# A residual block on one core: head blocks through the weight buffers, left columns first, three staggered chunks, later border transposes

## The chip, the core and the metric

One NeuronCore of a Trainium2 chip runs the whole block in one launch. The metric is the device time of one execution in microseconds. TensorE (PE in the profile) does matmuls and transposes, VectorE (DVE) and ScalarE (ACT) move, scale and convert, SyncE (SP) issues most DMAs, GpSimd (POOL) a few.

## What is computed

One layer for 256 tokens, model width 1024, all in float32 (the reference, cut):

```python
h = rmsnorm(x, ffn1_pre_g);  x = x + 0.5 * rmsnorm(swiglu(h, ffn1_w_in, ffn1_w_down), ffn1_post_g)
h = rmsnorm(x, mix_pre_g)
q_a, f_a, i_a, g_a, q_b, k_b, v_b, f_b, gates = split(h @ w_in)
o_a = rmsnorm(hgrn2_chunkwise(q_a, f_a, i_a), hg_norm_g) * silu(g_a)   # gated linear recurrence
o_b = fox_attention(q_b, k_b, v_b, f_b + fox_f_bias)                    # causal, forget gates
gate = sigmoid(gates + b_gate)
y = gate[0] * (o_a @ w_branch_a) + gate[1] * (o_b @ w_branch_b)
x = x + rmsnorm(y @ w_out, mix_post_g)
x = x + rmsnorm(mem_cross_attention(rmsnorm(x, mem_pre_g), rmsnorm(mem, mem_kv_g)), mem_post_g)
h = rmsnorm(x, ffn2_pre_g);  x = x + 0.5 * rmsnorm(swiglu(h, ffn2_w_in, ffn2_w_down), ffn2_post_g)
```

The inner width of each FFN is 2816, taken as 11 chunks of 256 (`NFF`).

## The kernel before

Every float32 operand of a large matmul is split into a rounded part `hi` (ScalarE cast, L122) and the rest `lo` (VectorE subtraction, L123), and each product is three matmuls: hi by hi, hi by lo, lo by hi. The weights are 261 units of 128 x 1024. `unit` loads one through SP into a `raw` buffer (four of them) and converts it into a pair `hi`/`lo` (eight pairs); it does so once and keeps the pair in a cache, so a pair stays held until its last matmul. `chunk` is four units, one 1024 x 512 piece of a matrix. `loads` lists the weight DMAs in the order they are written.

`proj_tok` multiplies 128 tokens (half `h`) by a chunk: 24 matmuls of 512 columns into one bank (tag `mm`, two banks). `rows_proj` and `down` accumulate a half of the tokens over rows of a weight into two banks of 512 columns each (tag `acc`, four banks); the results of `accs`, `po` are for token halves 0 and 1. The token halves go one after the other so that work on one lies under the matmuls of the other:

- `post` ends a sublayer for one half: sums of squares by ScalarE (`ssq`, L219), the product with the post gain (L279), an inverse root by an integer start value and Newton steps on 128 x 1 tiles (`rstd_of`, L203 to L210), and the update of `x` (L283).
- `half` follows it: eight PE transposes of the new `x` (`to_T`, L256), their gain and hi/lo split (`gain_split`, L247 and L248), and the pre-norm's inverse root. `half(X2, ...)` stands at the border from FFN 1 to the projections, `half(X3, ...)` from the mixer's output to the memory sublayer, `half(X4, ...)` from the memory output to FFN 2.
- In an FFN, `act_evac` makes a chunk's activations (L308, L310) and `flush` transposes and splits them (L303, L136, L137) for `down`. `STAG` is the number of last chunks whose `down` runs after all activations, half 0 and then half 1.

The tile framework orders each engine's queue by its own model of when operands are ready; the order then is fixed and each engine works it off in order. `after(i)` gives a block high priority but puts it on PE behind matmul number `i` of the list `log`; the constants `L_...` say how many matmuls behind the start of a stage. `issue_after` alone does this for one instruction, DMA issues included. These constants are lower limits: a block comes later if the model has it ready later.

At the head, x^T comes in five DMAs on ACT's queue into tiles of its own and the first four units through `unit` on SP's queue; `act_first` runs the first two FFN chunks for both halves, k-block by k-block, before the inverse root of `x` is known (`norm_1`). Seven matmuls on ones (`WARM`) run before data is there.

Of the kernel before, what the change touches and what calls it, by code (L numbers as in the profile page):

```python
# [16 lines left out]
P = 128  # L17
# [27 lines left out]
WARM = 7  # L45

X_AT = 6
# [18 lines left out]
def block_kernel(ctx: ExitStack, tc: tile.TileContext, wts, x_in, xT_in, mem_in, memT_in, cols, rows, fbias, masks, out):  # L66
# [46 lines left out]
    def unit(name, i, parts=1):  # L113
        u = _AT[name] + i
        if u not in cache:
            raw = wp.tile([P, D], F32, tag="raw", name=nm("raw"), bufs=4)
            hi = wp.tile([P, D], F32R, tag="hi", name=nm("hi"), bufs=8)
            lo = wp.tile([P, D], F32R, tag="lo", name=nm("lo"), bufs=8)
            for a in range(0, D, D // parts):
                cut = slice(a, a + D // parts)  # L120
                loads.append(nc.sync.dma_start(raw[:, cut], wts[u][:, cut]).ins)
                S.copy(hi[:, cut], raw[:, cut])  # L122
                V.tensor_tensor(out=lo[:, cut], in0=raw[:, cut], in1=hi[:, cut].bitcast(F32), op=ALU.subtract)  # L123
            cache[u] = (hi, lo)
        return cache[u]
# [74 lines left out]
    def rstd_of(s, scaled=True):  # L200

        v = s1(name="v")
        V.tensor_scalar(out=v, in0=s[:, 0:1], scalar1=s[:, 1:2], scalar2=D * EPS, op0=ALU.add, op1=ALU.add)  # L203
# [11 lines left out]
        V.tensor_scalar(out=r, in0=y, scalar1=-1.0 / 256.0, scalar2=None, op0=ALU.mult)  # L215
        return r
# [55 lines left out]
    def post(ps, h, grow, factor=1.0, last=False):  # L272

        s = s1(2, name="ss2")
        ts = []
        for j in range(2):
            ssq(s[:, j : j + 1], ps[j])
            t = sp.tile([P, 512], F32, tag="z2", name=nm("post"), bufs=3)
            V.scalar_tensor_tensor(out=t, in0=ps[j], scalar=-factor / 256.0, in1=grow[:, j * 512 : (j + 1) * 512], op0=ALU.mult, op1=ALU.mult)  # L279
            ts.append(t)  # L280
        r = rstd_of(s, scaled=False)
        for j, (t, xh) in enumerate(zip(ts, x_halves(h))):
            V.scalar_tensor_tensor(out=xh, in0=t, scalar=r, in1=xh, op0=ALU.mult, op1=ALU.add)  # L283
            if last:
                nc.sync.dma_start(out[h * P : (h + 1) * P, j * 512 : (j + 1) * 512], xh)


    def ffn(w_in, w_dn, X, r2, n_tok, i_row, first_half, second_half=None):
# [17 lines left out]
        def act_evac(ps, c, h):  # L306
            sg = sp.tile([P, FC], F32, tag="c1", name=nm("sg"), bufs=7)
            S.activation(sg, ps[:, :FC], AF.Silu, scale=r2[h])  # L308
            a = sp.tile([P, FC], F32, tag="c1", name=nm("at"), bufs=7)
            V.scalar_tensor_tensor(out=a, in0=ps[:, FC:], scalar=r2[h], in1=sg, op0=ALU.mult, op1=ALU.mult)  # L310
            ats[c, h] = a
            if h == 1:
                late.append(c)
# [19 lines left out]
        def down(c, h):  # L333
            act = acts[c]
            hs = slice(h * P, (h + 1) * P)
            for j in range(2):
                wh, wl = unit(w_dn, 2 * c + j)
                ah, al = act[:, 0, j, hs], act[:, 1, j, hs]
                for n in range(2):
                    ns = slice(n * 512, (n + 1) * 512)  # L340
                    for i, (a, w) in enumerate(((ah, wh), (ah, wl), (al, wh))):
                        MM(accs[h][n], a, w[:, ns], start=(c == 0 and j == 0 and i == 0), stop=(c == NFF - 1 and j == 1 and i == 2))
# [21 lines left out]
        for c in range(n_tok, NFF):  # L364
# [10 lines left out]
            while done < min(c - 1, NFF - STAG):  # L375
# [4 lines left out]
                done += 1  # L380
        m = len(log)
        for c in range(NFF - STAG, NFF):
            down(c, 0)
# [3 lines left out]
        for c in range(NFF - STAG, NFF):  # L387
            down(c, 1)
        if first_half:
            first_half(m)  # L390
            post(accs[1], 1, grow, 0.5)
        else:
            post(accs[1], 1, grow, 0.5, True)
# [4 lines left out]
    xT = [m4([P, 2, T + 1], n="xT") for _ in range(KB // 2)]  # L398
    for kb in range(2):
        S.dma_start(xT[0][:, kb], xT_in[:, kb])  # L400
    for j in range(1, 4):
        S.dma_start(xT[j], xT_in[:, 2 * j : 2 * j + 2])
# [350 lines left out]
    def gates(c):  # L753
# [3 lines left out]
        nc.sync.dma_start(brow, rows[4 + c // 2, c % 2 * 512 : c % 2 * 512 + 512].partition_broadcast(P))  # L757
# [43 lines left out]
    last = None  # L801
    for c in range(2):
        ua, ub = chunk("br_a", c), chunk("br_b", c)
        for h in range(2):
            za, zb = zs[c][:, h], zs[2 + c][:, h]
            m = len(log)
            pa = mm()
            proj_tok(pa, OA, ua, h)
            if last:
                y_T(*last, m + L_Y)  # L810
            V.tensor_tensor(out=za, in0=pa, in1=za, op=ALU.mult)
            pb = mm()
            proj_tok(pb, OB, ub, h)
            V.tensor_tensor(out=zb, in0=pb, in1=zb, op=ALU.mult)
            V.tensor_tensor(out=za, in0=za, in1=zb, op=ALU.add)
            last = c, h

    def rows_proj(ps, X, name, h, kbs):
        a, b = h * P, h * P + P
        for kb in kbs:  # L820
            wh, wl = unit(name, kb)
            for n in range(2):
# [8 lines left out]
    for h in range(2):  # L831
        rows_proj(po[h], Y, "w_out", h, range(0, 4))
        if h == 0:
            y_T(*last, m + L_Y)
# [5 lines left out]
    half(X3, r3, 0, G_MEM, m + L_WO)  # L840
# [5 lines left out]
    for c in range(2):  # L846
# [8 lines left out]
        if c == 0:  # L855
            half(X3, r3, 1, G_MEM, m + L_MK)
# [74 lines left out]
    for h in range(2):  # L931
        m = len(log)
# [14 lines left out]
def _layout(inputs):  # L947
# [41 lines left out]
    def col(v):  # L989
# [12 lines left out]
    )  # L1002
    r = {
        "wts": wts, "x": nat(a["x"]), "xT": np.concatenate([tra(a["x"]), col(a["ffn1_pre_g"][0])[:, :, None]], axis=2), "mem": nat(a["mem"]), "memT": tra(a["mem"]),
# [19 lines left out]
```

## Time and profile before

| | |
|---|---|
| runs | 807.54, 808.13, 808.2 us, median 808.13 |
| profiled execution | 807.36 us, span 805.6 us |
| granted TensorE clock, mean over the span | 0.997 |
| busy: PE, DVE, ACT | 98%, 65%, 51% of the span |
| HBM read | 146.02 MB, 183 GB/s over the span |
| a weight unit, 512 KB, from issue to landing | 4.3 us median |

The span runs from the first to the last instruction of the program that the profiler recorded; the execution's own time is a little longer. Rows of the timeline give start and duration in us, engine, source line, operation, output and inputs, shape and count; a bracket tells how long the engine sat idle before and what released it. Matmuls overlap, so a row's duration is not its share of the time: the distance between starts is.

### The profile page before, as it was taken

The page shows a single profiled execution, that of the slowest core. Times are in us where ns is not written, and L with a number is a line of the kernel's source. Part 1 is how long each engine was busy: PE and PEld are TensorE (multiplying, and loading weights), DVE is VectorE, ACT ScalarE, POOL GpSimd, SP SyncE. Part 2 cuts the span into 40 slices and gives each one's busy share as a digit, 9 for nine tenths or more (in the row PEclk, how much of TensorE's full clock was granted, in tenths as well). Part 3 has the DMA queues.
Part 4 walks back from the last instruction along what each step waited for, and adds up shares of the span by engine and source line. Part 5 has one row for each costly group of instructions (what it writes and reads, how often), then busy time and mean ns, then how long its engine had stood idle before and what let it go on. Part 6 is the DMA issues. An engine that isn't in the chain of part 4 may idle for free.

```text
span 805.6 us, 12769 instructions
## 1 busy us (share of the span) xinstructions
PE 792.6 (98%) x5040; PEld 679.4 (84%) x5040; DVE 525.1 (65%) x837; ACT 414.3 (51%) x623; POOL 9.2 (1%) x20
## 2 busy tenths in 40 slices
PE   8999999999999999999999999999999999999996
PEld 6888888888899889998888888999887788888884
DVE  6865545548776897678675666975659655545544
ACT  6754444537754435447674445645647654434531
POOL 0000000000000100200000000000000000000000
PEclk9999999999999999999999999999999999999998
DMA  8866654555455463643486555455425656665521
GB/s 331 302 223 209 211 200 157 193 173 183 164 203 171 171 195 123 212 155 120 139 291 235 177 161 201 146 197 196 151 77 186 210 185 206 209 201 166 182 79 52
DMA packets 41867, 147.90 MB, mean 184 GB/s; under 512 B 4808, under 2 KB 5200, under 8 KB 41808
## 3 DMA queue, kind: packets, MB, share of 16 engines
q1 hardware_dynamic: 40624, 144.46, 53.2%
q0 software_dynamic: 464, 1.58, 0.6%
q10 hardware_dynamic: 720, 1.05, 0.4%
q8 instruction: 39, 0.64, 0.3%
q14 instruction: 20, 0.16, 0.1%
HBM read 146.02 MB, written 1.06 MB: 183 GB/s over the span
## 4 chain that ended last, share of the span: by engine, by line
PE 89%; DVE 4%; DMA 2%; issue 2%; ACT 1%; SPq 0%; DVEq 0%; ACTq 0%
PE mm L80 63%; PE acc L80 23%; DMA raw<-in_wts_dram 2%; DVE lo L123 2%; PE tr L303 1%; PE tr L80 1%; ACT junk L219 1%; DVE xs L283 1%; PE tr L256 1%; DVE t L208 1%; DVE y L210 0%; ACT hi L122 0%; PE tr L712 0%; DVE post L279 0%; PE tr L901 0%
## 5 line engine op out<-in xcount | busy, mean ns | idle before, releaser
L123 DVE TENSOR_TENSOR lo<-raw,hi 128x1024 fp32r<-128x1024 f32 (+1 forms) x262 | 317.7, 1222 | 93.3 <-ACT hi L122 83.7
L122 ACT CAST hi<-raw 128x1024 fp32r<-128x1024 f32 (+1 forms) x262 | 270.8, 1047 | 140.0 <-PE mm L80 105.1
L80 PE MATMUL mm<-lo,hT 128*128 128x512 f32 x576 | 225.9, 392 | 0.0
L80 PE MATMUL mm<-hi,hT 128*128 128x512 f32 x576 | 225.6, 392 | 0.0
L80 PE MATMUL mm<-hi,lT 128*128 128x512 f32 x576 | 225.1, 391 | 0.1
L80 PEld LDWEIGHTS mm<-hi,lT 128*128 128x128 f32 x576 | 108.2, 188 | 23.0 <-DVE lT L248 0.8
L80 PEld LDWEIGHTS mm<-hi,hT 128*128 128x128 f32 x576 | 108.2, 188 | 22.6 <-ACT hT L247 0.5
L80 PEld LDWEIGHTS mm<-lo,hT 128*128 128x128 f32 x576 | 108.2, 188 | 21.7
L80 PE MATMUL acc<-hi,act 128*128 128x512 f32 x352 | 111.8, 391 | 0.0
L80 PE MATMUL mm<-hT,lo 128*128 128x256 f32 x392 | 111.3, 284 | 0.0
L80 PE MATMUL mm<-hT,hi 128*128 128x256 f32 x392 | 111.2, 284 | 0.0
L80 PE MATMUL mm<-lT,hi 128*128 128x256 f32 x392 | 111.1, 283 | 0.0
L80 PEld LDWEIGHTS acc<-hi,act 128*128 128x128 f32 x352 | 66.1, 188 | 13.4
L80 PEld LDWEIGHTS mm<-lT,hi 128*128 128x128 f32 x392 | 75.2, 192 | 0.1
L80 PEld LDWEIGHTS mm<-hT,hi 128*128 128x128 f32 x392 | 75.2, 192 | 0.1
L80 PEld LDWEIGHTS mm<-hT,lo 128*128 128x128 f32 x392 | 75.2, 192 | 0.1
L80 PE MATMUL acc<-lo,act 128*128 128x512 f32 x176 | 70.0, 398 | 0.0
L308 ACT ACTIVATE sg<-mm,rstd 128x256 f32<-128x256 f32 x40 | 19.0, 474 | 76.2 <-PE mm L80 76.2
L310 DVE SCALAR_TENSOR_TENSOR at<-mm,rstd,sg 128x256 f32<-128x256 f32 x40 | 19.2, 480 | 58.8 <-ACT sg L308 58.8
L80 PEld LDWEIGHTS acc<-lo,act 128*128 128x128 f32 x176 | 33.1, 188 | 6.4
L80 PE MATMUL acc<-hi,hT 128*128 128x512 f32 x96 | 35.5, 396 | 1.6 <-ACT hi L122 1.1
L80 PE MATMUL acc<-hi,lT 128*128 128x512 f32 x96 | 35.4, 396 | 0.5 <-DVE lT L248 0.5
(175 smaller groups left out, 630.2 us busy)
## 6 DMA issues: line engine op xcount, KB each, us to landing
raw<-in_wts_dram SPq DMA_DIRECT2D x260, 512.0 KB, 4.3
grow<-in_rows_dram SPq DMA_DIRECT2D x4, 512.0 KB, 5.8
brow<-in_rows_dram SPq DMA_DIRECT2D x4, 256.0 KB, 4.9
xs<-in_x_dram SPq DMA_DIRECT2D x2, 512.0 KB, 5.5
cbm<-cd POOLq DMA_DIRECT2D x2, 512.0 KB, 8.5
memT<-in_memT_dram SPq DMA_DIRECT2D x2, 512.0 KB, 7.5
ms<-in_mem_dram SPq DMA_DIRECT2D x2, 512.0 KB, 7.8
out_dram<-xs SPq DMA_DIRECT2D x4, 256.0 KB, 2.1
```

The source lines that it names most:

```text
L80: log.append(PE.matmul(*args, **kw).ins)
L122: S.copy(hi[:, cut], raw[:, cut])
L123: V.tensor_tensor(out=lo[:, cut], in0=raw[:, cut], in1=hi[:, cut].bitcast(F32), op=ALU.subtract)
L208: V.scalar_tensor_tensor(out=t, in0=v, scalar=y, in1=y, op0=ALU.mult, op1=ALU.mult)
L219: S.activation(junk[:, : src.shape[-1]], src, AF.Square, accum_out=dst)
L256: PE.transpose(ps[:, j * P : (j + 1) * P], src(kb), ident)
L283: V.scalar_tensor_tensor(out=xh, in0=t, scalar=r, in1=xh, op0=ALU.mult, op1=ALU.add)
L303: PE.transpose(trv[:, j, h * P : (h + 1) * P], ats[c, h][:, j * P : (j + 1) * P], ident)
L308: S.activation(sg, ps[:, :FC], AF.Silu, scale=r2[h])
L310: V.scalar_tensor_tensor(out=a, in0=ps[:, FC:], scalar=r2[h], in1=sg, op0=ALU.mult, op1=ALU.mult)
```

## The change

1. *Head.* x^T block, weight block and gain column of each of eight k-blocks stand side by side in a new input `head` (128 x 776 per block) and are loaded by eight DMAs on SP's queue through the four `raw` buffers. The unit list `wts` starts at unit 4. A block's `lo` is written behind its gain split. `WARM` is 8; the load of `x` moves behind another load (`X_AT`); the gate bias rows are loaded behind the gates' units.
2. *Inverse root.* Three Newton steps (six operations) become one Newton step and one of higher order (five), with another scale (`SC_RSTD`).
3. *FFN.* `STAG` is 3. For half 0 (and half 1 in FFN 2) the last chunks' `down` does columns 0 to 511 of all of them and then columns 512 to 1023. The flush in the first two chunks of FFN 2 goes; these chunks are flushed in chunk 2.
4. *The end.* `post_last`: ScalarE's square root and VectorE's reciprocal with one Newton step; the table of the square root is called for behind the last Silu; the last 512 columns are updated and stored in two pieces, one over ACT's queue.
5. *Branches.* `br_a` for both halves, then `br_b` for both halves, per 512 columns.
6. *Memory sublayer.* `half(X3, ...)` for half 0 moves from the end of the output projection into the key projection. The memory output does k-blocks 0 to 2 for both halves, then the rest of half 0 (left columns first), then the rest of half 1.
7. Larger `L_...` constants.

```diff
+SC_RSTD = 0.375
-STAG = 4
-L_ACT = 15
-L_F1 = 18
-L_IA = 22
-L_WO = 18
-L_MK = 46
-L_MO = 18
+STAG = 3
+L_ACT = 21
+L_F1 = 24
+L_IA = 36
+L_WO = 30
+L_MK = 84
+L_MO = 21
-WARM = 7
-X_AT = 6
+WARM = 8
+X_AT = 10
...
-        for c in (3.0, 12.0, 768.0):
-            t = s1(name="t")
-            V.scalar_tensor_tensor(out=t, in0=v, scalar=y, in1=y, op0=ALU.mult, op1=ALU.mult)
-            y2 = s1(name="y")
-            V.scalar_tensor_tensor(out=y2, in0=t, scalar=c, in1=y, op0=ALU.subtract, op1=ALU.mult)
-            y = y2
+        t = s1(name="t")
+        V.scalar_tensor_tensor(out=t, in0=v, scalar=y, in1=y, op0=ALU.mult, op1=ALU.mult)
+        z = s1(name="y")
+        V.scalar_tensor_tensor(out=z, in0=t, scalar=3.0, in1=y, op0=ALU.subtract, op1=ALU.mult)
+        t = s1(name="t")
+        V.scalar_tensor_tensor(out=t, in0=v, scalar=z, in1=z, op0=ALU.mult, op1=ALU.mult)
+        w = s1(name="t")
+        V.scalar_tensor_tensor(out=w, in0=t, scalar=40.0 / 3.0, in1=t, op0=ALU.subtract, op1=ALU.mult)
+        y = s1(name="y")
+        V.scalar_tensor_tensor(out=y, in0=w, scalar=80.0, in1=z, op0=ALU.add, op1=ALU.mult)
...
+    def post_last(ps, h, grow, factor):
+        s = s1(2, name="ss2")
+        ts = []
+        for j in range(2):
+            ssq(s[:, j : j + 1], ps[j])
+            if j == 0:
+                sums = s1(name="v")
+                V.tensor_scalar(out=sums, in0=s[:, 0:1], scalar1=D * EPS, scalar2=None, op0=ALU.add)
+            else:
+                y = s1(name="y")
+                S.activation(y, s[:, 1:2], AF.Sqrt, bias=sums)
+                v = s1(name="v")
+                V.tensor_tensor(out=v, in0=s[:, 1:2], in1=sums, op=ALU.add)
+            t = sp.tile([P, 512], F32, tag="z2", name=nm("post"), bufs=3)
+            V.scalar_tensor_tensor(out=t, in0=ps[j], scalar=-factor * 16.0, in1=grow[...], op0=ALU.mult, op1=ALU.mult)
+            ts.append(t)
+        z = s1(name="y")
+        V.reciprocal(z, y)
+        t = s1(name="t")
+        V.scalar_tensor_tensor(out=t, in0=v, scalar=z, in1=z, op0=ALU.mult, op1=ALU.mult)
+        r = s1(name="y")
+        V.scalar_tensor_tensor(out=r, in0=t, scalar=3.0, in1=z, op0=ALU.subtract, op1=ALU.mult)
+        for a, b, eng in ((0, 512, nc.sync), (512, 768, nc.scalar), (768, 1024, nc.sync)):
+            xh = xs[:, h, a:b]
+            V.scalar_tensor_tensor(out=xh, in0=ts[a // 512][...], scalar=r, in1=xh, op0=ALU.mult, op1=ALU.add)
+            eng.dma_start(out[h * P : (h + 1) * P, a:b], xh)
...
+            if c == NFF - 1 and h == 1 and not first_half:
+                with tc.issue_after(silu.ins):
+                    S.activation(warm, ones[:, 0:1], AF.Sqrt)
...
             for c in range(n_tok):
-                n = len(log)
                 act_tok(c, h)
-                flush(n + L_ACT)
...
-        for c in range(NFF - STAG, NFF):
-            down(c, 0)
+        for cut in (left, right):
+            for c in range(NFF - STAG, NFF):
+                down(c, 0, (cut,))
...
-    xT = [m4([P, 2, T + 1], n="xT") for _ in range(KB // 2)]
-    for kb in range(2):
-        S.dma_start(xT[0][:, kb], xT_in[:, kb])
-    for j in range(1, 4):
-        S.dma_start(xT[j], xT_in[:, 2 * j : 2 * j + 2])
+    heads = [wp.tile([P, D], F32, tag="raw", name=nm("head"), bufs=4) for _ in range(KB)]
+    for kb in range(KB):
+        loads.append(nc.sync.dma_start(heads[kb][:, : T + 512 + KB], head_in[kb]).ins)
...
-    for j in range(4):
-        unit("f1_in", j, 2 if j == 0 else 1)
-        for i in range(2):
-            gain_split(X1, 2 * j + i, xT[j][:, i, :T], xT[j][:, i, T:], first=2 * j + i == 0)
+    for kb in range(KB):
+        if kb % 2 == 0:
+            cache[_AT["f1_in"] + kb // 2] = parts_of()
+        hi, lo = (p[:, kb % 2 * 512 : kb % 2 * 512 + 512] for p in cache[_AT["f1_in"] + kb // 2])
+        w = heads[kb][:, T : T + 512]
+        S.copy(hi, w)
+        gain_split(X1, kb, heads[kb][:, :T], heads[kb][:, T + 512 + kb : T + 512 + kb + 1], first=kb == 0)
+        V.tensor_tensor(out=lo, in0=w, in1=hi.bitcast(F32), op=ALU.subtract)
...
-        nc.sync.dma_start(brow, rows[...].partition_broadcast(P))
+        with tc.issue_after(loads[-1]):
+            nc.sync.dma_start(brow, rows[...].partition_broadcast(P))
...
-    half(X3, r3, 0, G_MEM, m + L_WO)
...
-        if c == 0:
-            half(X3, r3, 1, G_MEM, m + L_MK)
+            if c == 0:
+                half(X3, r3, j, G_MEM, m + (L_WO, L_MK)[j])
...
-    for h in range(2):
-        m = len(log)
-        rows_proj(po[h], AO, "mo", h, range(0, 4))
-        rows_proj(po[h], AO, "mo", h, range(4, 8))
-        if h == 1:
-            half(X4, r4, 0, G_F2, m + L_MO)
-        post(po[h], h, g3)
+    for kb in range(3):
+        for h in range(2):
+            rows_proj(po[h], AO, "mo", h, (kb,))
+    for n in range(2):
+        rows_proj(po[0], AO, "mo", 0, range(3, KB), (n,))
+    post(po[0], 0, g3)
+    m = len(log)
+    rows_proj(po[1], AO, "mo", 1, range(3, KB))
+    half(X4, r4, 0, G_F2, m + L_MO)
+    post(po[1], 1, g3)
```

More of the change, by code (lines that the diff above doesn't have):

```diff
@@ L65, in block_kernel @@
 @with_exitstack
[L66 removed]
+def block_kernel(ctx: ExitStack, tc: tile.TileContext, wts, head_in, x_in, mem_in, memT_in, cols, rows, fbias, masks, out):
     nc = tc.nc
@@ L111, in block_kernel, with parts_of, unit @@
     loads = []
-    def unit(name, i, parts=1):
+    def parts_of():
+        return [wp.tile([P, D], F32R, tag=t, name=nm(t), bufs=8) for t in ("hi", "lo")]
+    def unit(name, i):
         u = _AT[name] + i
@@ L116, in unit @@
             raw = wp.tile([P, D], F32, tag="raw", name=nm("raw"), bufs=4)
[L117 to L123, printed above, removed]
+            hi, lo = parts_of()
+            loads.append(nc.sync.dma_start(raw, wts[u - 4]).ins)
+            S.copy(hi, raw)
+            V.tensor_tensor(out=lo, in0=raw, in1=hi.bitcast(F32), op=ALU.subtract)
             cache[u] = (hi, lo)
@@ L270, in load_row, with post @@
         return r
-    def post(ps, h, grow, factor=1.0, last=False):
+    def post(ps, h, grow, factor=1.0, store=False):
         s = s1(2, name="ss2")
@@ L386, in ffn @@
         m = len(log)
-        for c in range(NFF - STAG, NFF):
-            down(c, 1)
         if first_half:
+            for c in range(NFF - STAG, NFF):
+                down(c, 1)
             first_half(m)
@@ L821, in rows_proj @@
             wh, wl = unit(name, kb)
-            for n in range(2):
+            for n in cols:
                 ns = slice(n * 512, (n + 1) * 512)
```

66 lines of the change are left out of this document (38 added, 28 removed).

## The prediction

> **What bounds the kernel now.** I read the page first, then the chain in order of time, then the timeline of each stretch where TensorE is not back to back.
>
> ```profile
> span 805.6 us, 12769 instructions
> PE 792.6 (98%) x5040; PEld 679.4 (84%) x5040; DVE 525.1 (65%) x837; ACT 414.3 (51%) x623; POOL 9.2 (1%) x20
> ```
>
> TensorE carries the time. The chain shows its pace in a steady piece of the second FFN:
>
> ```profile
> 652.52 10.88 PE mm L80 x48
> 667.03 0.44 PE tr L303 x4
> ```
>
> 48 matmuls of 512 columns in 10.88 us are 0.227 us each, with no wait between. The change alters the number of real matmuls nowhere, so it can win only where PE waits: at the head, at the borders between stages, and behind the last matmul. It loses where it makes a new wait.
>
> **The head.** Eight k-blocks of x^T and weights are fetched; each wants six matmuls (1.36 us) in chunk 0.
>
> ```profile
> 1.68 1.73 ACTq L402 DMA_DIRECT2D xT<-in_xT_dram  x3
> 4.68 0.35 DVE L245 TENSOR_SCALAR hT<-xT 128x256 fp32r<-128x256 f32 x1 [3.66 <-DMA xT<-in_xT_dram]
> 4.84 0.60 ACT L122 CAST hi<-raw 128x512 fp32r<-128x512 f32 x1
> 5.49 0.72 PE L80 MATMUL acc<-hi,hT 128*128 128x512 f32 x2 [1.07 <-ACT hi L122]
> 6.56 0.51 ACT L247 ACTIVATE hT<-xT 128x256 fp32r<-128x256 f32 x1
> 6.69 0.69 DVE L123 TENSOR_TENSOR lo<-raw,hi 128x512 fp32r<-128x512 f32 x1 [0.53 <-ACT hi L122]
> 7.30 0.48 DVE L248 SCALAR_TENSOR_TENSOR lT<-xT,hT 128x256 fp32r<-128x256 f32 x1
> 29.59 0.39 PE L80 MATMUL mm<-hi,hT 128*128 128x512 f32 x1
> ```
>
> The first two chunks are 96 matmuls, 21.8 us at pace. They take 29.59 - 5.49 = 24.1 us, so 2.3 us are lost inside and the stream behaves as if it had started at 7.8 us.
>
> ```profile
> 0.00:14.00 14.00, 10.91 (x42) 7.92 (x43) 6.81 (x13) 8.06 (x14) 0.71 (x6) 1.00 0.84 308
> DMA to landing us min/median/max: 3.2/4.7/7.0
> ```
>
> These are the first 14 us by windows (last column GB/s) and the landing times of the weight tile in the first 60 us. A new block is 128 rows of 776 floats, 397 KB: 1.29 us at 308 GB/s, under the 1.36 us that PE needs for it. When does block 0 land? It is issued at about 0.75 like the first load now. The fastest 512 KB load took 3.2 us, so 3.95 is the early bound; the first piece of x^T and the first half unit, together about as many bytes, were in by 4.84, the late bound. I take 4.4. Per block ACT then has 0.60 + 0.51 = 1.11 us and DVE 0.48 + 0.69 = 1.17 us, both under 1.36. Followed through: block 0 makes PE start at 5.1; block 1 lands at 5.7, its hi and hT are done at 6.8, lT at 7.35, lo at 8.05, so its matmuls end at 8.5; from block 2 on (in at 7.0, ready at 8.1) PE is the slower party. Matmul 13 starting at 8.5 means an effective start of 8.5 - 12 x 0.227 = 5.8, against 7.8: 2.0 us. Blocks 4 to 7 must wait until a raw buffer is read out by lo (block 0: about 6.0) and need a fresh trip of about 3.2 us: in at 9.3, hT at 10.4, wanted at 11.2. Later ones have less air, so I book 0.2 us back: **head -1.8** (range -2.5 to 0). The extra warm-up matmul lies before the first landing: nothing. The bias row's transfer leaves the head for the gates stage: nothing, since its load there follows that chunk's last unit and its reader comes after 24 matmuls, 5.4 us.
>
> **The borders.** Each residual update (`post`) and its transposes must hide under the matmuls of the other token half.
>
> ```profile
> 172.60:181.20 8.60, 8.60 (x40) 7.13 (x39) 1.66 (x2) 0.59 (x1) 0.00 (x0) 1.00 0.46 158
> 182.20:204.90 22.70, 21.77 (x102) 17.39 (x101) 20.70 (x50) 15.05 (x30) 0.00 (x0) 1.00 0.56 186
> 589.00:597.10 8.10, 8.10 (x37) 6.71 (x36) 0.56 (x1) 0.00 (x0) 0.00 (x0) 1.00 0.05 20
> 597.15:621.00 23.85, 23.60 (x113) 19.41 (x112) 21.18 (x51) 17.69 (x35) 0.00 (x0) 1.00 0.52 177
> ```
>
> DVE (third number behind the length) idles before the border, 1.66 of 8.60 and 0.56 of 8.10 us, and is then the full engine, 20.7 of 22.7 and 21.2 of 23.9. The reason is the pool: eight hi/lo pairs are all held by the four staggered chunks (or by all of the memory output weights), so the next stage's conversions run only once the second half gives them back.
>
> ```profile
> L123 DVE TENSOR_TENSOR lo<-raw,hi 128x1024 fp32r<-128x1024 f32 x8 | 9.8, 1219 | 0.2 <-ACT hi L122 0.2
> L279 DVE SCALAR_TENSOR_TENSOR post<-acc,grow 128x512 f32<-128x512 f32 x4 | 2.8, 689 | 8.1 <-ACT junk L219 7.9
> 202.81 0.39 PE L80 MATMUL mm<-hi,lT 128*128 128x512 f32 x1
> 203.92 1.32 PE L256 MATMUL tr<-ident,xs 128*128 128x128 f32 x8 [0.72 <-DVE xs L283]
> 188.22 0.63 PE L256 MATMUL tr<-ident,xs 128*128 128x128 f32 x4 [0.20 <-issue]
> 503.58 0.63 PE L256 MATMUL tr<-ident,xs 128*128 128x128 f32 x4 [0.23 <-DVE xs L283]
> 603.94 0.63 PE L256 MATMUL tr<-ident,xs 128*128 128x128 f32 x4 [0.25 <-DVE xs L283]
> 621.89 0.40 PE L80 MATMUL mm<-lo,hT 128*128 128x512 f32 x1
> 624.80 0.40 PE L80 MATMUL mm<-lo,hT 128*128 128x512 f32 x1
> 636.57 0.39 PE L80 MATMUL mm<-lo,hT 128*128 128x512 f32 x1
> 637.64 0.44 PE L303 MATMUL tr<-ident,at 128*128 128x128 f32 x2 [0.69 <-DVE at L310]
> ```
>
> *FFN 1 to the projection.* Waits 0.20 and 203.92 - 202.81 - 0.23 = 0.88. Three staggered chunks shorten the second half from 48 to 36 matmuls: 12 x 0.227 = 2.7 us of cover gone. Off DVE go two of the eight `lo` (2 x 1.22, into the idle stretch), one of the first half's two `post` products (0.69, since its left 512 columns now finish 18 matmuls early) and one small operation in each of three root chains (0.22 each by the tail's rows below): 3.8 us. It comes out 1.1 us ahead: **-1.0** (range -1.1 to +2.7). *Memory border.* The transposes are put at least 30 matmuls into the key projection, its 192 matmuls being the cover: **-0.2** (0 to -0.25). *Memory output to FFN 2.* Waits 0.25, then nine steps in 2.91 us from 621.89 (0.87 lost behind the second half's splits), then 637.64 - 636.57 - 0.23 = 0.84 for an activation that DVE delivers late. Interleaving k-blocks 0 to 2 leaves 30 instead of 48 matmuls behind the first half, 4.1 us of cover gone; three `lo` (3.7), a `post` product (0.7) and the root chains (0.66) leave DVE's full stretch, 5.1. So the 0.25 goes and about 0.3 of the 0.87; the rest stays, since those transposes are still placed four matmuls before that cover ends. The flush at 637.64 moves a chunk later, behind 21 matmuls of new work, and its 0.84 goes: **-1.4** (-2.0 to +4.1).
>
> *Stagger and flush order:* chunk 7's down projection moves into the loop, the same matmuls. Left columns first leaves chunk 10's activations only 12 matmuls, 2.7 us, and its transposes as cover:
>
> ```profile
> 775.92 1.59 PE acc L80 x7
> 775.96 0.47 ACT L308 ACTIVATE sg<-mm,rstd 128x256 f32<-128x256 f32 x1 [0.33 <-PE mm L80]
> 777.81 0.59 ACT L136 CAST act<-tr 128x512 fp32r<-128x512 f32 x1 [0.44 <-PE tr L303]
> 616.84 1.28 ACT L308 ACT_TABLE_LOAD   x1 [2.92 <-DVE rstd L215]
> 618.14 0.47 ACT L308 ACTIVATE sg<-mm,rstd 128x256 f32<-128x256 f32 x1
> ```
>
> The cast is done at 778.4, 2.5 us after the tail's first matmul: it fits. In FFN 2 a square-root table load follows that `sg` (ends 776.43): 1.28 and a one-column warm-up (estimated 0.2 from the one-column read of 0.19 in the tail's rows) end at 777.9, 0.1 behind the cast's present start. Nothing (0 to +0.3 each).
>
> One piece of the branch stage in the chain:
>
> ```profile
> 450.36 10.93 PE mm L80 x48
> ```
>
> The branch stage now works weight by weight with the same matmuls and transposes. There PE runs at pace already (48 in 10.93 us), and four units at a time instead of eight leave more air: nothing, to -0.1.
>
> Against the table load the Trainium skill speaks: "ScalarE: Activation LUTs", What ACT_TABLE_LOAD costs, puts a switch at 1283 ns plus a drain of 1380 ns. The row here agrees with the first part and shows no drain behind it, the next activation starting 0.02 us after the load.
>
> **The tail.**
>
> ```profile
> 797.40 0.60 ACT L219 ACTIVATE junk<-acc 128x512 f32<-128x512 f32 x1 [9.51 <-PE acc L80]
> 798.61 0.19 ACT L219 ACTIVATION_READ_ACCUMULATOR junk<-acc 128x1 f32 x1
> 799.45 0.20 DVE L203 TENSOR_SCALAR v<-ss 128x1 f32<-128x1 f32 x1
> 801.22 1.42 DVE L283 SCALAR_TENSOR_TENSOR xs<-post,y,xs 128x512 f32<-128x512 f32 x2
> out_dram<-xs SPq DMA_DIRECT2D x4, 256.0 KB, 2.1
> ```
>
> The second half's sum is read at 798.80 either way, because it waits for the last matmul. Now DVE does `post`, then eight small operations from 799.45 to 801.2, then two updates until 802.64, and the last store leaves there. After: `post` as now, `v` and three small operations at about 0.22 us, while the square root runs on ACT beside `post`: updates from about 800.3. They come in 512, 256 and 256 columns, about 1.5 us, so the last store leaves at 801.8 and carries 128 KB instead of 256. That is 0.85 sooner, and 0 to 0.4 for the smaller store: **-1.0** (-0.6 to -1.3).
>
> **Sum.** Head 1.8, borders 1.0 + 0.2 + 1.4, tail 1.0: 5.4 us. The profiled execution took 807.36 us (span 805.6 and 1.8 around it); the median of the runs is 808.13. So 807.36 - 5.4 = 802.0 for that execution and, 0.77 above it, **802.7** for the median.
>
> **Rivals.** (1) *The raw ring paces the head.* Four buffers serve a block in trip + conversion. With the median trip of 4.7 instead of 3.2, block 4 is in at 10.7, ready at 11.9 instead of 11.2, and the next chunk's first unit a round later again behind; about 1.8 us return, and the time is 804.5. For it: the large trips of this stretch. Against: those had four x^T pieces and up to four units in flight at once, where now there are at most four smaller blocks. (2) *The cover is cut and DVE does not get lighter*, because the queue orders the next stage's conversions into the border all the same. Then 2.7 + 4.1 = 6.8 us of cover are missing, the waits of 0.88, 0.20, 0.25 and 0.87 stay, and head, tail, memory border and flush save 3.8: 811.1. It is slower by over 0.2% once more than 5.4 of the 6.8 come back. For it: DVE at nine tenths there, with 2.0 and 2.7 us of air. Against: two long idle stretches right before, with the loads free to come. (3) *The table switch holds ACT for two load lengths*, 2.56 us: the cast starts 1.4 late at 779.2 and is done at 779.8; the matmul that wants it is due 12 matmuls and two transposes behind 775.92, at 778.8: 1.0 us, 803.7. The page named above, in the Trainium skill, would say this. (4) *Several shortfalls at once* leave no difference.
>
> **How the numbers follow.** Forecast 0.66; ring 0.15; cover 0.09; table 0.04; no difference 0.06. About 0.2%, 1.6 us, is what a measurement of this kernel can tell from none. Faster takes the forecast, ring and table: 0.85; same 0.06; slower 0.09. With every term at its good end the forecast reaches 800.6; upward the range takes in the ring (804.5), the table and another 1.2 us of a border's lost cover: 805.6.
>
> **What would show it.** First real matmul near 5.1 and the 97th near 27.8; no wait over 0.2 us at the transposes behind FFN 1 and none at the first flush of FFN 2; `lo` in the stretches that now idle; from the last sum read (798.80) to the end of the span 5.8 instead of 6.8 us. I am wrong if PE waits on landings between 9 and 20 us, or on `xs` and `lT` behind the shortened halves.

## The result, and the profile after

The changed kernel takes **802.62 us** (median of four runs, 801.96 to 803.17) against 808.16 us beside it, a ratio of 0.9931 with a 95% interval of 0.9914 to 0.9949. Run again later it took 802.62 us once more (five runs, 801.98 to 803.86, ratio 0.9933, 0.9920 to 0.9945). The forecast was 802.7 us. The profiled execution took 801.96 us, its span is 800.2 us; 5.4 us of span are gone, as the sum had it, but two of its terms missed in opposite directions.

First the page of the changed kernel:

```profile
span 800.2 us, 12768 instructions
PE 791.5 (99%) x5042; PEld 680.3 (85%) x5042; DVE 520.6 (65%) x819; ACT 416.8 (52%) x629; POOL 8.4 (1%) x20
```

PE is busy 1.1 us less and the span is 5.4 us shorter: what went is waiting. Where it went shows when the start of the n-th PE instruction, counted from the first real matmul, is compared in both traces (5,026 of them in each):

| stretch (PE instruction) | before, us | after, us | difference | forecast |
|---|---|---|---|---|
| span start to the first | 5.49 | 4.50 | -0.99 | |
| first to 97th | 24.10 | 23.03 | -1.07 | |
| 97th to 193rd | 20.50 | 21.23 | +0.73 | |
| head, sum | | | **-1.33** | -1.8 |
| 193rd to 1101st, FFN 1 and its border | 186.15 | 184.99 | **-1.16** | -1.0 |
| 1101st to 3461st, mixer | 264.21 | 264.21 | 0.00 | 0 |
| 3461st to 3701st, memory border | 30.35 | 30.25 | **-0.10** | -0.2 |
| 3701st to the last matmul, memory output and FFN 2 | 266.79 | 264.96 | **-1.83** | -1.4 |
| last matmul to the end | 8.00 | 7.02 | **-0.98** | -1.0 |

*Head.* The timeline of PE, ACT and DVE in the changed kernel:

```profile
4.50 1.10 PE L81 MATMUL acc<-hi,hT 128*128 128x512 f32 x2
27.53 0.62 PE L81 MATMUL mm<-hi,hT 128*128 128x512 f32 x2
26.21 1.05 ACT L123 CAST hi<-raw 128x1024 fp32r<-128x1024 f32 x1 [0.64 <-DMA raw<-in_wts_dram]
27.30 1.23 DVE L124 TENSOR_TENSOR lo<-raw,hi 128x1024 fp32r<-128x1024 f32 x1 [0.29 <-ACT hi L123]
28.57 0.50 PE L81 MATMUL mm<-lo,hT 128*128 128x512 f32 x1 [0.42 <-DVE lo L124]
```

The first matmul is at 4.50 (forecast 5.1), the 97th at 27.53 (27.8). But one matmul further PE waits: 28.57 - 27.76 = 0.81, 0.58 over pace. Read upwards, the matmul waits for `lo`, `lo` for `hi`, and the cast for the transfer, the last in the chain. So the third chunk's first weights land late. The windows, here from 8 to 14 and 14 to 28 us, say since when; first the kernel before, then the changed one:

```profile
8.00:14.00 6.00, 5.05 (x20) 3.34 (x21) 4.10 (x7) 5.00 (x9) 0.00 (x0) 1.00 1.04 412
14.00:28.00 14.00, 14.00 (x63) 11.57 (x62) 13.54 (x33) 11.57 (x20) 0.00 (x0) 1.00 0.94 358
```

```profile
8.00:14.00 6.00, 6.00 (x27) 4.76 (x26) 4.63 (x10) 4.38 (x9) 0.00 (x0) 1.00 0.89 295
14.00:28.00 14.00, 13.98 (x61) 10.99 (x60) 9.74 (x27) 9.46 (x17) 0.00 (x0) 1.00 0.94 350
```

From 8 to 14 us the transfers run at 295 GB/s instead of 412 (last column), 117 x 6 us = 0.70 MB less. PE is busy there all the time (6.00 of 6.00), so little shows until 14 us later: between 9 and 20 us no matmul starts more than 0.18 us over pace (the largest is at 17.42). That would be the first rival's cause, with its effect not where I looked for it; the last two experiments test it.

*Borders.* In the changed kernel, by windows (behind the length the busy time of PE, PEld, DVE, ACT and POOL, then clock, DMA share and GB/s) and by groups of DVE from 187 to 202 and from 601 to 617.5 us:

```profile
173.00:186.00 13.00, 13.00 (x60) 10.57 (x59) 6.93 (x12) 5.58 (x10) 0.00 (x0) 1.00 0.46 161
186.60:203.20 16.60, 16.56 (x81) 13.30 (x80) 15.25 (x40) 11.81 (x28) 0.00 (x0) 1.00 0.54 191
591.00:600.20 9.20, 9.20 (x42) 7.62 (x41) 3.17 (x4) 2.43 (x5) 0.00 (x0) 1.00 0.43 161
600.20:618.30 18.10, 18.07 (x89) 14.74 (x87) 16.85 (x47) 13.05 (x28) 0.00 (x0) 1.00 0.41 145
L124 DVE TENSOR_TENSOR lo<-raw,hi 128x1024 fp32r<-128x1024 f32 x6 | 7.2, 1218 | 0.0
L124 DVE TENSOR_TENSOR lo<-raw,hi 128x1024 fp32r<-128x1024 f32 x5 | 6.1, 1220 | 0.0
```

Six `lo` are left in the first border and five in the second, where before there were eight each; the stretches ahead, in which DVE had 1.66 of 8.60 and 0.56 of 8.10 us to do, now hold 6.93 of 13.00 and 3.17 of 9.20. The windows differ in length: as long a stretch of the kernel before holds 4.57 (169.20 to 182.20) and 1.29 us (588.00 to 597.20). Followed one by one, the first two `lo` of the projections start at 174.49 and 176.44 instead of 184.76 and 186.23, and the first three of FFN 2 at 588.24, 590.98 and 593.70 instead of 600.43, 601.90 and 604.37. DVE is as full as before in the shorter stretch (15.25 of 16.60), and PE no longer feels it. The transposes:

```profile
188.99 1.03 PE L261 MATMUL tr<-ident,xs 128*128 128x128 f32 x8
201.71 1.03 PE L261 MATMUL tr<-ident,xs 128*128 128x128 f32 x8
513.86 0.66 PE L261 MATMUL tr<-ident,xs 128*128 128x128 f32 x4 [0.37 <-DVE lT L253]
604.20 1.29 PE L261 MATMUL tr<-ident,xs 128*128 128x128 f32 x8
617.45 1.03 PE L261 MATMUL tr<-ident,xs 128*128 128x128 f32 x8
635.09 0.60 PE L336 MATMUL tr<-ident,at 128*128 128x128 f32 x4
641.02 0.60 PE L336 MATMUL tr<-ident,at 128*128 128x128 f32 x4
```

No bracket stands behind FFN 1, behind the memory output or at the first two flushes of FFN 2 (635.09 and 641.02), where the kernel before had 0.20, 0.72, 0.25 and 0.69. One bracket is new, in the memory border.

*Tail*, in order of time (ACT, then DVE):

```profile
794.15 0.19 ACT L224 ACTIVATION_READ_ACCUMULATOR junk<-acc 128x1 f32 x1
794.38 0.29 ACT L303 ACTIVATE y<-ss,v 128x1 f32<-128x1 f32 x1
794.38 0.69 DVE L307 SCALAR_TENSOR_TENSOR post<-acc,grow 128x512 f32<-128x512 f32 x1 [3.33 <-ACT junk L224]
795.05 0.16 DVE L310 RECIPROCAL y<-y 128x1 f32<-128x1 f32 x1
795.70 1.54 DVE L317 SCALAR_TENSOR_TENSOR xs<-post,y,xs 128x512 f32<-128x512 f32 x3
```

From the sum's end (794.34) to the first update 1.36 us, against 801.22 - 798.80 = 2.42 before.

### The profile page after: what moved, and what is told of

Same layout as the page of the kernel before. It is cut to its first block, busy times and chain, and to the rows that moved or that the text cites. A ratio compares the mean times of both kernels' runs of the same rounds, so it can differ in the third digit from the quotient of the medians.

```text
span 800.2 us, 12768 instructions
## 1 busy us (share of the span) xinstructions
PE 791.5 (99%) x5042; PEld 680.3 (85%) x5042; DVE 520.6 (65%) x819; ACT 416.8 (52%) x629; POOL 8.4 (1%) x20
## 3 DMA queue, kind: packets, MB, share of 16 engines
HBM read 146.05 MB, written 1.06 MB: 184 GB/s over the span
## 4 chain that ended last, share of the span: by engine, by line
PE 93%; DVE 2%; DMA 2%; ACT 1%; issue 1%; SPq 0%; DVEq 0%; ACTq 0%
PE mm L81 65%; PE acc L81 24%; PE tr L336 1%; DMA head<-in_head_dram 1%; PE tr L81 1%; DMA raw<-in_wts_dram 1%; PE tr L261 1%; DVE lo L124 1%; DVE lT L253 0%; ACT junk L224 0%; PE tr L753 0%; DVE post L284 0%; PE tr L839 0%; PE tr L942 0%; DVE lo L452 0%
## 5 line engine op out<-in xcount | busy, mean ns | idle before, releaser
L124 DVE TENSOR_TENSOR lo<-raw,hi 128x1024 fp32r<-128x1024 f32 x257 | 312.5, 1225 | 128.0 <-ACT hi L123 119.5
L123 ACT CAST hi<-raw 128x1024 fp32r<-128x1024 f32 x257 | 266.5, 1051 | 168.7 <-PE mm L81 102.0
```

The source lines that it names most:

```text
L123: S.copy(hi, raw)
L124: V.tensor_tensor(out=lo, in0=raw, in1=hi.bitcast(F32), op=ALU.subtract)
```

## Experiments

Each is the changed kernel with one thing altered. The run's median says little below 1 us, because the head varies from execution to execution; behind the 193rd matmul unaltered stretches agree mostly within 0.06 us between traces; the mixer differs by up to 0.2, in one of them by 0.39, and the tail in one by 0.37. From there to the end the changed kernel takes 751.44 us, in its second profile 751.49, and the kernel before 755.49. So each alteration is judged in its own stretch.

### Parts undone: head, stagger, memory output, flush

The old head (x^T apart, first units in the ring, seven warm-ups, old `X_AT`):

```diff
-    heads = [wp.tile([P, D], F32, tag="raw", name=nm("head"), bufs=4) for _ in range(KB)]
+    xT = [m4([P, 2, T + 1], n="xT") for _ in range(KB // 2)]
...
+        unit("f1_in", j, 2 if j == 0 else 1)
```

> The changed kernel with the old head alone: x^T in five loads on ACT's queue, units 0 to 3 through the unit function, seven warm-up matmuls, the load of x behind load 6. Theory (the head gives its share by PE starting earlier and not stalling inside the first 96 matmuls, of which 0.6 us is lost again to a late weight unit in chunk 2): 1.4 us slower than the changed kernel, first real matmul at 5.5 us, the 97th at 29.6, no wait at 28 us. Rival (what counts is the bias row that no longer loads at the head, not the blocks through the raw buffers; that row stays late here): the 97th matmul at 28.5 or sooner, under 0.7 us slower.

804.06 us (803.77 to 805.89). First matmul 5.26, 97th 29.87 (the rival with the bias row had 28.5 or sooner), 193rd 50.37, and 97th to 193rd is 20.50 again. The new head is what gained, and what gives 0.73 back is part of it. How much it gained depends on the execution that it is held against: 1.61 us against the changed kernel's first profile (48.76), 0.91 against the median of the eight profiles here that have the same head code (49.46, from 48.66 to 52.71). Of the 1.44 us between the medians of the times, 0.48 lie behind the 193rd matmul in the profiles, where nothing was altered, 0.37 of them in the tail.

Four staggered chunks again (`STAG = 4`):

> The changed kernel with four staggered chunks instead of three in both FFNs. Theory (with three, two weight pairs are free during the first half, so two conversions leave the border, and that outweighs 12 matmuls of cover): eight conversions between 182 and 204 us again, the transposes of the second half wait about 0.7 us on xs again; 0.2 to 0.8 us slower. Rival (the cover is what counts, the relief is small): 0.2 to 0.6 us faster.

803.12 us (802.85 to 803.91). 193rd to 1101st +0.61 (-0.19 up to the 871st, +0.80 behind it). Eight `lo` start from 184.15 to 199.03 us again, and the wait is back at the second transposes, with 0.36 by the bracket instead of the 0.7 that I expected; this kernel's row:

```profile
202.31 1.32 PE L261 MATMUL tr<-ident,xs 128*128 128x128 f32 x8 [0.36 <-DVE xs L288]
```

The memory output in its old order, one half and then the other:

> The changed kernel with the old order of the memory output: all of half 0, then all of half 1. Theory (three weight pairs freed early take three conversions out of the border, worth more than 18 matmuls of cover): eight conversions between the end of half 0 and the second transposes, waits there of 0.25 and up to 0.9 us again; 0.3 to 1.0 us slower. Rival (the gain at this border comes from the later flush alone; longer cover would help): same within 0.2 us or up to 0.5 us faster.

804.19 us (801.87 to 806.79). 3701st to the last +0.63, but not where I expected it: no bracket stands at the transposes (604.29 and 621.55 here). The time goes behind the second ones: the 26 steps from the 4236th to the 4262nd start lose 0.95 us over pace, in the changed kernel 0.29, in the kernel before 1.09. That is the stretch of the prediction's 0.87. Nothing else differs by over 0.2, but its profiled head is 3.95 us later than the changed kernel's with the same code (193rd matmul at 52.71).

The early flush in FFN 2:

```diff
             for h in range(2):
+                n = len(log)
                 act_tok(c, h)
+                flush(n + 15)
```

> The changed kernel with the flush of FFN 2's first two chunks back inside their own loop, 15 matmuls behind the start of each. Theory (PE waits for an activation that DVE delivers late, behind a weight conversion): a wait of 0.5 to 0.9 us at the transposes of chunk 1, 0.5 to 0.9 us slower. Rival (with DVE lighter at this border the activation is in time anyway): under 0.2 us slower.

803.63 us (802.69 to 804.53); 3701st to the last +1.65, twice what I expected. ACT, DVE and PE in this kernel:

```profile
631.96 1.05 ACT L123 CAST hi<-raw 128x1024 fp32r<-128x1024 f32 x1 [1.74 <-DMA raw<-in_wts_dram]
632.91 0.47 ACT L341 ACTIVATE sg<-mm,rstd 128x256 f32<-128x256 f32 x1
633.04 1.23 DVE L124 TENSOR_TENSOR lo<-raw,hi 128x1024 fp32r<-128x1024 f32 x1 [1.56 <-ACT hi L123]
634.18 0.48 DVE L346 SCALAR_TENSOR_TENSOR at<-mm,rstd,sg 128x256 f32<-128x256 f32 x1
634.71 0.44 PE L336 MATMUL tr<-ident,at 128*128 128x128 f32 x2 [1.25 <-DVE at L346]
```

The transposes wait for `at`. Its `sg` is done at 633.38, but `at` starts at 634.18, without a break behind a `lo` on DVE's queue. That `lo` waits for its cast, the cast for its weights, and `sg` stands behind the same cast on ACT's queue: an activation that PE wants is late because of a transfer that it has nothing to do with. Counted from the 3701st start, PE reaches this point 0.8 us sooner than in the kernel before and the transposes start only 0.3 sooner, so the same order costs more than the 0.84 of before.

### The end

The old end for the last half, with the new five-operation root (`post` instead of `post_last`, no early table):

> The changed kernel with the old end: one routine for both output halves, three Newton steps after the sum, two stores, and no square-root table loaded early. Theory (the tail's 1.0 us is the shorter chain behind the last sum): from the last matmul's start to the end of the span 8.0 us as in the kernel before, instead of 7.0; time about 803.6. Rival (the tail gained because left columns are finished first, which this kernel keeps, and not by the chain): the stretch stays at 7.4 us or less, time under 803.1.

804.58 us (803.92 to 806.98); last matmul to the end 7.81 us, +0.79. `post` starts at 796.02, the first update at 798.14: 2.12 us instead of 1.32. The 0.19 still missing to the old 8.00 goes with the sixth operation, which this kernel lacks: from `v` to the first update it takes 1.52 us instead of 801.22 - 799.45 = 1.77.

The square root's table loaded only where it is needed:

```diff
-                with tc.issue_after(silu.ins):
-                    S.activation(warm, ones[:, 0:1], AF.Sqrt)
```

> The changed kernel without the early one-column square root, so the table is loaded where the tail first needs it, behind the last sum. Theory (a load costs the 1.28 us that its row shows and nothing behind it): the square root ends at 1.28 us later, of which 0.4 is covered by the second product on DVE (in the changed kernel the root is done 0.4 us before the reciprocal starts), so the tail is 0.8 to 0.9 us longer, time about 803.5. Rival (the switch holds ACT for two load lengths, third rival of the prediction): the tail 2.1 to 2.3 us longer, time about 804.8. If the load was no matter at all: no difference.

804.37 us (803.53 to 807.31); the tail is 0.94 us longer. ACT and DVE in this kernel:

```profile
794.77 0.19 ACT L224 ACTIVATION_READ_ACCUMULATOR junk<-acc 128x1 f32 x1
794.98 1.28 ACT L303 ACT_TABLE_LOAD   x1
796.27 0.29 ACT L303 ACTIVATE y<-ss,v 128x1 f32<-128x1 f32 x1
796.60 0.16 DVE L310 RECIPROCAL y<-y 128x1 f32<-128x1 f32 x1 [0.85 <-ACT y L303]
```

The load takes 1.28 us, starts 0.02 behind the reading of the sum (794.96), and the root starts 0.01 behind the load. The Trainium skill, "ScalarE: Activation LUTs", What ACT_TABLE_LOAD costs, adds a drain of about 1380 ns to each load. The trace has none of it on the path, where it would show, and DVE's idle time is 0.85 and not the 2.2 that one would estimate with it. In the changed kernel the early load lies at 777.34 to 778.62, and the cast that the third rival saw delayed starts at 778.74, its matmuls without a wait.

### Root and memory border

Three Newton steps of two operations again (scale 1/256):

> The changed kernel with the old reciprocal square root of three Newton steps of two DVE operations (six) instead of two steps in five. Theory (one operation of 0.22 us less in each of the chains behind the sums, at the borders only partly seen because the transposes have waits of their own): 0 to 0.6 us slower, the new waits at the FFN 1 and the memory border 0.2 us longer each. Rival (the chain is not on the path at the borders): no difference there, waits unchanged.

804.88 us (804.47 to 805.17). From the 193rd matmul to the end 752.71, **+1.28**: +0.55 in FFN 1's border, -0.22 in the memory border, +0.93 from the memory output on. Two rows of DVE from the first border, and the waits of PE at the first and the last border:

```profile
188.82 1.23 DVE L124 TENSOR_TENSOR lo<-raw,hi 128x1024 fp32r<-128x1024 f32 x1
189.96 1.41 DVE L284 SCALAR_TENSOR_TENSOR xs<-post,y,xs 128x512 f32<-128x512 f32 x2
190.81 0.63 PE L257 MATMUL tr<-ident,xs 128*128 128x128 f32 x4 [0.20 <-issue]
607.07 0.63 PE L257 MATMUL tr<-ident,xs 128*128 128x128 f32 x4 [0.25 <-DVE xs L284]
```

One operation of 0.22 us in a chain of 128 x 1 tiles puts the update, and with it the transposes, behind other work that DVE has queued: here the root is done at 188.90 and a `lo` comes before the update, where in the changed kernel the root is done at 187.41 and the update starts at 187.44. My bound of 0.6 was too low. The memory border, for which I had expected 0.2 more, takes less, and why is not shown.

The memory border's transposes at their old places:

> The changed kernel with the memory border's transposes at their old places (18 and 46 matmuls into the work behind, and not inside the branch loop). Theory (that deeper placing took away a wait of 0.38 and met another of about the same size): the stretch from the 3461st to the 3701st PE instruction within 0.2 us of the changed kernel's 30.25, its wait back at its old place; time within 0.3 of the changed kernel's. Rival (the deeper place itself brought the new wait and a better place lies between): 0.3 us or more faster there. Rival of the other side (the cut cover of this border is what the deeper place pays for): slower there by 0.5 us or more.

803.26 us (802.68 to 803.78); the stretch differs by -0.03. The move is worth nothing: the changed kernel has the wait of 0.37 for `lT` in the row at 513.86. The old wait that I expected back in its place did not come (no bracket at 500.65 and 512.79), so what takes the time there instead is not shown.

### What gives back part of the head

Masks and a constant loaded in FFN 1 instead:

> The changed kernel with the loads of the masks (224 KB) and of a small constant moved out of the first 20 us, to chunk 6 of FFN 1. Theory (the 0.7 us that the head gives back between its 97th and 193rd matmul come from the third chunk's weights queueing behind 1.3 MB of other loads): those weights land about 0.6 us sooner (224 KB at 350 GB/s), the wait at 28 us shrinks from 0.58 over pace to under 0.2, matmuls 97 to 193 take 20.6 to 20.8 us instead of 21.23, time about 802.1. Rival (what is late is the conversion on ACT and DVE, not the landing): 21.1 us or more, no difference.

803.93 us (803.73 to 804.93). 193rd matmul at 51.65, 97th to 193rd 22.37, with a wait of 1.2 for `lo`: not faster. How much slower it is stays open, since 51.65 lies within what the unaltered head shows (48.66 to 52.71). 224 KB less in the queue did not help: the theory was incomplete.

The changed kernel once more, and two with the last four head blocks outside the ring, ran next. First the unaltered one:

> The changed kernel once more, unaltered, beside the two below on the same chip, because its head differed from execution to execution in the traces so far (the 193rd matmul at 48.7 to 52.7 us with the same code). Theory: median 802.5 to 803.6, ratio to the kernel before 0.993 to 0.9955; the 193rd matmul anywhere between 48.7 and 50.5.

802.62 us; 193rd matmul at 50.56 in the profile, 1.8 later than in the first and just outside the range that I expected. From 8 to 14 us 254 GB/s, and two waits at the third chunk, of 0.80 and 0.53.

Head blocks 4 to 7 in buffers of the data pool:

```diff
-    heads = [wp.tile([P, D], F32, tag="raw", name=nm("head"), bufs=4) for _ in range(KB)]
+    heads = [wp.tile([P, D], F32, tag="raw", name=nm("head"), bufs=4) if kb < 4 else m4([P, D], F32, "head") for kb in range(KB)]
```

> The changed kernel with only the first four head blocks in the raw ring and the last four in buffers of the data pool that are still unused, so that no head block waits for another's conversion and the ring is free four units sooner. Theory (the four-buffer ring holds the transfers back between 8 and 14 us, 295 GB/s where the kernel before moved 412, and the bytes missing then are the late weights at 28 us): 8 to 14 us goes to 380 GB/s or more, the units of the third chunk land 1 us sooner or more, the wait at 28 us is gone, matmuls 97 to 193 take 20.5 us as in the kernel before, time 0.7 us or more below the unaltered kernel beside it and with a smaller spread. Rival (the transfers after 14 us, not the ring, set those landings): the same 21 us or more there and no difference. Rival of the other side (eight blocks in flight delay the first ones, as 12 pieces did in the kernel before): first matmul 0.5 us later or more, and no gain.

**809.0 us** (807.98 to 810.91), ratio 1.0008 (0.9999 to 1.0018): the whole gain lost. The first matmul is late and nothing is gained, as the last rival has it, but for another reason. DVE and PE in this kernel, and two windows:

```profile
10.51 0.69 DVE L452 TENSOR_TENSOR lo<-head,hi 128x512 fp32r<-128x512 f32 x1 [0.30 <-ACT hi L450]
11.12 0.35 DVE L250 TENSOR_SCALAR hT<-head 128x256 fp32r<-128x256 f32 x1
11.61 1.19 PE L81 MATMUL acc<-hi,hT 128*128 128x512 f32 x2 [7.06 <-DVE hT L250]
11.50:17.50 6.00, 5.89 (x14) 4.62 (x15) 6.00 (x12) 5.31 (x10) 0.00 (x0) 0.50 0.78 285
17.70:24.00 6.30, 6.30 (x29) 5.18 (x28) 4.83 (x11) 4.82 (x10) 0.00 (x0) 0.99 1.01 376
```

The framework's order had put the first block's `hT`, needed by the first matmul, behind five `lo`, four of them of blocks that land later, so PE stood until 11.61, and then worked 6.1 us at a granted clock of 0.50 (matmuls 0.427 us apart). Two of the eleven runs show a mean granted clock of 0.999 over the span instead of 0.992 to 0.995 and took 809.00 and 809.52 us all the same, so the loss does not hang on the half clock. The run says nothing on the ring: the `raw` buffers were read out late too, and the first load behind the blocks is issued at 11.89.

So the same again, with blocks 4 to 7 in other buffers and the order held block by block:

```diff
+    heads = [wp.tile([P, D], F32, tag="raw", name=nm("head"), bufs=4) if kb < 4 else wp.tile([P, D], F32, tag="lo", name=nm("head"), bufs=8) for kb in range(KB)]
...
+        with (tc.issue_after(last) if last else ExitStack()):
             S.copy(hi, w)
             gain_split(...)
+        last = V.tensor_tensor(out=lo, in0=w, in1=hi.bitcast(F32), op=ALU.subtract).ins
```

> Four head blocks in the raw ring and four in buffers that the lower halves of later weights use, as the kernel before had separate places, and the order of each block's conversions held to block by block, so that the first blocks are not converted behind the fourth and fifth (which in the run with eight buffers kept the first matmul until 11.61 us). Theory (the ring holds the transfers back between 8 and 14 us, and the bytes missing then are the late weights at 28 us): 360 GB/s or more from 8 to 14 us, the 193rd matmul at 48.4 us or before instead of 48.7 to 50.6, no wait over 0.5 us near 28 us, time 801.0 to 802.2. Rival (the transfers after 14 us set those landings, ring or not): the 193rd matmul within the spread of the changed kernel's, time 802.3 to 803.6. Rival of the other side (eight blocks in flight delay the first four and the granted clock falls in the pauses): the 97th matmul behind 29 us, time above 803.6.

**801.67 us** (five runs, 801.51 to 801.90), ratio 0.9916 (0.9902 to 0.9929) to the kernel before: the best version here, 0.95 below the changed kernel, with a spread of 0.4 instead of 1.9; all five lie below all nine runs of that kernel. PE and the window, and then the loads that SP issues up to 15 us, first of the changed kernel and then of this one:

```profile
8.85 0.73 PE L81 MATMUL acc<-hi,hT 128*128 128x512 f32 x2 [0.81 <-ACT hT L252]
28.24 0.39 PE L81 MATMUL mm<-hi,hT 128*128 128x512 f32 x1
28.46 0.39 PE L81 MATMUL mm<-lo,hT 128*128 128x512 f32 x1
8.00:14.00 6.00, 5.19 (x23) 3.94 (x23) 5.17 (x11) 5.76 (x12) 0.00 (x0) 1.00 1.03 414
```

```profile
0.75 8.67 SPq L439 DMA_DIRECT2D head<-in_head_dram  x8
10.67 4.48 SPq L122 DMA_DIRECT2D raw<-in_wts_dram  x4
```

```profile
0.75 4.77 SPq L439 DMA_DIRECT2D head<-in_head_dram  x8
5.64 5.68 SPq L122 DMA_DIRECT2D raw<-in_wts_dram  x4
```

With the ring of four the eight blocks take until 9.42 us to be issued, since each of the last four waits for a buffer, and the first weights behind them go out at 10.67; here at 5.52 and 5.64. That is the ring holding the transfers back. 414 GB/s from 8 to 14 us, no wait at the third chunk, 97th to 193rd in 20.50. The other side's rival has its part too: with more blocks in flight the third lands at 7.75 instead of 6.31 us (7.16 in the changed kernel's second profile), PE waits 0.81 for it, and the 97th matmul comes at 28.24. The 193rd is then at 48.74, as in the first profile of the changed kernel. What is gained is that it comes there each time: the five times, less 1.77 around the span and 751.34 behind that matmul, put it at 48.4 to 48.8. The range for the 193rd matmul that I had put on record, 48.4 or before, was missed; the time and the rest were as expected. Two things are altered here, buffers and order. The changed kernel converts block by block too, only with a block's `lo` ahead of its `lT`, so the order is an unlikely cause; with four buffers it was not run by itself.

## Why the prediction came out, point by point

- **Sum.** Right to 0.1 us: 5.4 forecast, 5.40 in the span. Part of that is luck: the terms' errors cancel (the head 0.47 short, FFN 1's border 0.16 and the memory output 0.43 over), and the head is that of one execution. With the stretch behind the 193rd matmul fixed at 751.46 and 755.49 us, the medians put that matmul at 802.62 - 1.77 - 751.46 = 49.4 and 808.16 - 1.77 - 755.49 = 50.9 us (1.77 is the execution's time less its span): in a typical execution the head gives 1.5 and the rest 4.0.
- **Head, -1.8; measured -1.33 in the profile.** The first block landed at 3.57 us by the trace, before my early bound of 3.95; I had bounded a 397 KB transfer by a 512 KB one. It bought less than it seems: PE starts at 4.50 behind the eighth warm-up, and its second matmul, at 5.08, starts 0.35 over pace though its `hi` and `hT` were done by 4.22; what held it is not shown. Up to the 97th matmul I was 0.26 too low (2.06). The step that failed is the ring: I booked 0.2 us for blocks 4 to 7 and looked for waits from 9 to 20 us. There was none above 0.2, and block 4 landed at 8.87, before the 9.3 of the prediction. What the ring delayed were the loads behind the blocks, at 295 GB/s, and the bill came at 28 us, 0.73, and 1.8 and 3.95 us more in two other executions of the same head (50.56, 52.71 against 48.76). The first rival had the mechanism, "the next chunk's first unit a round later"; only its place and its size in the typical run were off.
- **FFN 1 border, -1.0; measured -1.16.** Both halves of the account are shown: undoing the stagger costs 0.61, undoing the root 0.55. Left columns first and the larger constants were not undone by themselves. The `lo` moved into the idle stretch as argued, and the second rival, that DVE gets no lighter, is refuted by the rows (six and five `lo`, not eight).
- **Memory border, -0.2; measured -0.10**, and none of it from the move (0.03). I took the old wait as gone without asking what is late next: it is `lT`, of an operand pair that DVE splits just then. What brought the 0.10 is not shown.
- **Memory output to FFN 2, -1.4; measured -1.83.** The step that was mis-sized is the 0.87 behind the second half's splits, of which I let only 0.3 go: by the 26 steps above 0.80 of 1.09 went. The wait of the flush is gone as forecast. Undone one at a time, order (0.63), flush (1.65) and root (0.93) add to more than 1.83, so they share waits: each is worth that only with the other two in place.
- **Tail, -1.0; measured -0.98.** The chain from the sum to the update is 1.06 shorter, the three updates take 0.12 more, and the smaller last store gave nothing: from the last update's end to the span's end 2.95 us in both kernels (805.59 - 802.64 and 800.19 - 797.24).
- **Nothing for branches, flush order and table:** mixer 0.00; the table load lies beside work, and by its row costs 0.94 where it does not.

## What to carry to other kernels

A buffer ring that a stream outgrows shows first in the windows' GB/s and only later, on another tile, as a wait: follow a late operand back to the transfer and then ask what the queue was doing ten us earlier. Freeing buffers helps only if the order of the engines stays: look at the first instructions of each queue before anything else. Where the start varies from run to run, compare traces by the n-th instruction of the bounding engine, and parts of a change can be told apart to 0.1 us in most stretches, to 0.4 in the worst case here.

## What was not expected of the hardware

- The same head code had its 193rd matmul anywhere from 48.66 to 52.71 us; with the ring of four the transfers ran at 254 to 295 GB/s from 8 to 14 us, with blocks 4 to 7 outside it and the order kept at 414. Why the transfers of one execution are slower than another's is left open.
- A pause of PE of 7.1 us was followed by 6.1 us at a granted clock of 0.50 (in the window; matmuls 0.427 us apart instead of 0.227). In the profile with the old memory output two waits of 1.21 and 1.06 us at the third chunk were followed by 3.4 us at 0.50 (31.50 to 34.90), which is part of why its 193rd matmul came at 52.71. The Trainium skill, "TensorE: Matmul & The Clock Gate", Part 1, has a half and a full rate and puts the way back at one or more busy windows of about 3.4 us, which run on regardless of when the kernel starts. The 6.1 us lie between one such window and two, so the run agrees.
- One 128 x 1 operation of 0.22 us more in each inverse root cost 1.28 us.
